# Four column groups at once in the conditioning beside the single tiles, and short vector steps of the attentions a quarter later in the order

## The chip, the cores and the metric

The kernel runs on one core of a Trainium2 chip. A core has a matrix engine (TensorE, PE in the profile, its weight loads as PEld), a vector engine (VectorE, DVE), an engine for activation functions (ScalarE, ACT), a general engine (GpSimd, POOL) and an engine that here only issues transfers (SyncE, SP). Each works through its own list of instructions in order and waits, where it must, on semaphores that the others raise. The metric is the device time of one execution in microseconds; the time before is the median of three.

## The reference

One inference step of a hybrid trunk with two layers and a model width of 2048, for 128 context tokens (`x_prompt`) and 512 latent tokens (`x_sample`) that share all weights. Cut to what matters here:

```python
def modulation(cond, w, b):                       # "conditioning": shift, scale, gate
    m = jax.nn.silu(cond) @ w + b                 # (2048) @ (2048, 6144), once for c and once for c_ctx
    return jnp.split(m, 3, axis=-1)

def rms_norm(x, g):
    return x * lax.rsqrt(jnp.mean(x * x, axis=-1, keepdims=True) + EPS) * g

for layer in range(2):
    sh, sc, gt = modulation(cond, ada_w[layer], ada_b[layer])
    h = rms_norm(x, norm_g[layer]) * (1.0 + sc) + sh
    x = x + gt * mixer(h)                         # even_mixer or odd_mixer

def even_mixer(h, ...):                           # one input projection, columns split in eight
    qa, ka, va, ga, ub, bb, cb, gb = split_cols(h @ w_in, EVEN_SPLIT)
    q, k = rms_norm(q_heads(qa), qn), rms_norm(kv_heads(ka), kn)
    o = banded_attend(apply_rope(q), apply_rope(k), v, k_ctx, v_ctx, sink)   # softmax with a sink logit
    y_a = o * silu(ga); y_b = bb * conv3(cb * ub) * silu(gb)
    return concat(y_a, y_b) @ w_out

def odd_mixer(h, ...):
    cq, ck, cv, cg, dq, dk, dv, dg = split_cols(h @ w_in, ODD_SPLIT)         # q, k: rms_norm, then rope
    o_c = rms_norm(attend(cq0, ck0, cv) - lam * attend(cq1, ck1, cv), c_on) * (1.0 - lam_init)
    y_c = o_c * silu(cg); y_d = attend(q_d, dk_all, dv_all) * silu(dg)
    return concat(y_c, y_d) @ w_out
```

The context tokens attend to themselves alone, the latent tokens to 256 cached keys and to the latent keys (in the even layer to a band of them). New keys and values of the context are outputs as well.

## The kernel before, in words

**Projections.** All activations lie transposed (features on partitions, 640 tokens along the row), each split in a high and a low part of a reduced type, and every product is three matmuls: high by high, low by high, high by low (lines 313 to 315, and 582 to 584 in the paired form). One "tile" is 128 columns of a weight matrix by 640 tokens, in two PSUM banks `pa` and `pb` of 320. Its 2048 contraction rows come in four "quarters"; a quarter is one 128x512 weight piece, loaded as `raw` by SP (line 291), split into `wh` by ACT and `wl` by DVE (`split`, lines 278 and 279), and used in 24 matmuls of 320 columns. Loads are issued five quarters ahead, splits three (`RAW_AHEAD`, `SPLIT_AHEAD`), in four buffers each.

**Stages.** A start (transposes of x, first conditioning, a lead of six tiles worked side by side), the even layer's single tiles, a tail of it with `ada_beside`, paired tiles (`run_pairs`), the output projection, the odd layer's front, its single tiles with the attentions of D and C, and its output projection.

**Slots.** After each quarter's matmuls `run_tiles` calls `slot`. It advances three kinds of generators, each by hand up to its next `yield`: `prep` (what follows a finished q, k or v tile: `q_gen`, `k_gen`, `v_gen`), `attn` (the attention of two heads: `pair_gen` for A and D, `diff_gen` for C), and `fill`, the conditioning of later use, at a `rate` of so many steps a slot. So a `yield` in a generator moves what follows it by one quarter, and the attention's short operations stand between the weight splits of the projection on the same engines.

**Planner.** What is written is a priority, not the final order: the framework's planner goes through the program with a cost for each instruction and gives each engine the first written instruction that it holds to be ready. An engine's list is then fixed. Two neighbours in the program can be apart on the engine, and where the planner's cost for an operation is too low, the engine stands at run time.

**What the change touches.** `ada_wide` (lines 233 to 250) computes conditioning of the even layer's time on DVE: 1024 columns by 16 row blocks, two multiply-adds (line 245) for each block of `ada_w`, which comes in by a 512 KB load (line 240), three buffers. `ada_on_dve` (lines 188 to 212) does the same in the odd layer in 256-column pieces (lines 204, 210). `ada_beside` (lines 252 to 275) does two blocks of 512 columns on PE while the last single tiles of the even layer run: the 16 row blocks are products with 32 columns of weights, and row block kt goes to column group kt % 4 of the array (`tile_position=(0, 32 * g)`), so that the four groups give four partial sums that are added after a transpose. Before the change a step loads two row blocks (512 KB, `w8`, four buffers) and issues two matmuls, groups 0 and 1 or groups 2 and 3.

`soft` (line 757) makes a softmax's numerators: maximum (L759), exponential with its sum `l` (L766), and the reciprocal `rl` of the sum (L772). `pair_gen` scales the numerators by it on ACT (L852) before the transposes `pt_group` (L780); `diff_gen` mixes two maps into one on DVE (L1508, L1509). `k_gen` norms and rotates a key tile: squares on ACT, mean on DVE (L655), power -0.5 on POOL (L656), products on DVE (L657 to L668), transposes back (L612 and, for the cached keys, L676). `q_gen` rotates a query tile (L702 to L705) and takes its sum of squares (L709 to L720), the power of which (L726) is used as the scale of the exponential. At the end of `diff_gen` stands the output norm: L1528 to L1535, then the transposes of `on` (L1541).

Of the kernel before, what the change touches and what calls it, by code (L numbers as in the profile page):

```python
# [20 lines left out]
P = 128  # L21
D = 2048
KT = D // P
# [26 lines left out]
FILL0 = 2.05  # L50
# [5 lines left out]
def trunk_kernel(ctx: ExitStack, tc: tile.TileContext, I: dict, O: dict):  # L56
# [30 lines left out]
    V.memset(half, -0.5)  # L87
# [100 lines left out]
    def ada_on_dve(blocks, tags, parts=1, tie=lambda: None):  # L188
# [4 lines left out]
        for l, cb in blocks:  # L193
# [3 lines left out]
            if mark is not None:  # L197
                for c in range(2):
                    V.tensor_copy(acc[c][:, 0:1], mark)
            for i in range(KT * parts):  # L200
                kt, h = i % KT, i // KT
                w = ap.tile([P, wd], F32, tag=wt[i % 3], name="adaw", bufs=bufs)
                c0 = cb * 512 + h * wd
                nc.sync.dma_start(w, I["ada_w"][l, kt * P:(kt + 1) * P, c0:c0 + wd])
# [28 lines left out]
    def ada_wide(twins):  # L233

        for l, cb in twins:
            ap = pools["cur"]
            acc = [ap.tile([P, 1024], F32, tag=f"acc{c}", name=f"acc{c}", bufs=1) for c in range(2)]
            for kt in range(KT):
                w = ap.tile([P, 1024], F32, tag="adaw", name="adaw", bufs=3)
                nc.sync.dma_start(w, I["ada_w"][l, kt * P:(kt + 1) * P, cb * 512:(cb + 2) * 512])  # L240
                for c in range(2):
# [10 lines left out]
    def ada_beside(blocks):  # L252

        for l, cb in blocks:
            acc = pS.tile([P, 1024], F32, tag="S", name="adaS")
            for k0 in range(0, KT, 2):
                w = big("w8", bufs=4).rearrange("p (k n) -> p k n", k=2)
                nc.sync.dma_start(w, ada_src(l, cb, k0, 2))
                yield
                for kt in (k0, k0 + 1):  # L260
                    g = kt % 4
                    PE.matmul(acc[32 * g:32 * g + 32, 0:512], sT[:, kt, :], w[:, kt % 2, :],
                              start=(kt < 4), stop=(kt >= KT - 4), tile_position=(0, 32 * g))
# [362 lines left out]
    def k_gen(ap, pp, tag, src, gain, new_out, vals=None, then=None):  # L626
# [28 lines left out]
        V.tensor_scalar(ss, ss, 1.0 / P, EPS, ALU.mult, ALU.add)  # L655
        G.tensor_tensor(r, ss, half[:, 0:5], op=ALU.pow)  # L656
        V.tensor_mul(kg, kg, r[:, :, None].to_broadcast([P, 5, P]))  # L657
# [12 lines left out]
        yield  # L670
# [22 lines left out]
    def q_gen(ap, pp, tag, gain, then=None, wait=True):  # L693
# [795 lines left out]
    def diff_gen(ap, h, v, kq):  # L1489
# [284 lines left out]
```

## Time and profile before

| | us |
|---|---|
| median of three runs | 2297.72 |
| lowest and highest | 2293.41, 2299.14 |
| the profiled execution, its time | 2295.01 |
| the profiled execution, its span | 2293.2 |
| PE busy in it | 2245.8 |
| DVE, ACT, POOL busy | 1685.5, 1109.8, 196.1 |

The span runs from the first to the last instruction that the profiler saw; 1.8 us of the execution's time lie around it. Busy time is the union of an engine's instructions. A group of instructions is named by its line in the kernel, engine, operation and tiles; "waits" give the time that one engine stood idle before an instruction, and which instruction ended that. A matmul's record is longer than the distance at which the next one starts, because they are pipelined, so what a matmul costs the engine is read from the distance of starts.

### The profile page before, as it was taken

Reading aid. Unit: us, or ns where it says so; the run is one execution under the profiler, and the core shown is the slowest. Engines: PE = TensorE matmul, PEld = TensorE weight load, DVE = VectorE, ACT = ScalarE, POOL = GpSimd, SP = SyncE. Lnnn points to the kernel's source line nnn. Section 1 sums busy time; section 2 is a strip of 40 time slices with the busy share of each in tenths; the row PEclk is TensorE's granted clock in tenths of the full one; section 3 lists DMA queues with packets and bytes.
Section 4 is the critical chain, followed back from the end, with each engine's and each line's share of the span. In section 5 each row is a group of like instructions: output and inputs, shape, how many; then the busy total and the mean of one; then the engine's idle time right before and its main releaser. Section 6 shows DMA issues by size and latency. Waiting matters only on the chain.

```text
span 2293.2 us, 41410 instructions
## 1 busy us (share of the span) xinstructions
PE 2245.8 (98%) x15760; PEld 2156.4 (94%) x15760; DVE 1685.5 (73%) x3188; ACT 1109.8 (48%) x2269; POOL 196.1 (9%) x273
## 2 busy tenths in 40 slices
PE   7999999999999999999999999999999999999999
PEld 5888999999889999999999999999998998999999
DVE  4659999986747778878786664857758777677665
ACT  4335553545334445444644445566665554544343
POOL 2220000000000000000100000000000101111001
PEclk9999999999999999999999999999999999999999
DMA  9985656653642325744673334422324234237541
GB/s 358 339 285 157 187 154 210 181 173 120 208 150 89 98 87 192 238 138 125 227 225 112 106 118 136 136 65 86 108 74 148 78 114 125 78 106 252 159 138 49
DMA packets 387400, 351.45 MB, mean 153 GB/s; under 512 B 17906, under 2 KB 341968, under 8 KB 386688
## 3 DMA queue, kind: packets, MB, share of 16 engines
q1 hardware_dynamic: 373360, 298.15, 42.6%
q0 software_dynamic: 12976, 48.41, 5.9%
q8 instruction: 124, 2.03, 0.3%
q10 hardware_dynamic: 864, 2.23, 0.3%
q14 instruction: 76, 0.62, 0.1%
HBM read 305.86 MB, written 42.86 MB: 152 GB/s over the span
## 4 chain that ended last, share of the span: by engine, by line
PE 84%; DVE 7%; DMA 4%; ACT 2%; issue 2%; POOL 1%; SPq 0%; ACTq 0%; POOLq 0%; DVEq 0%
PE pq L583 10%; PE pq L584 10%; PE pq L582 10%; PE pa L313 6%; PE pa L314 6%; PE pb L314 6%; PE pb L313 6%; PE pa L315 6%; PE pb L315 6%; PE T L780 2%; DMA adaw<-in_ada_w 2%; PE S L792 1%; DVE acc L210 1%; PE S L794 1%; PE S L793 1%
## 5 line engine op out<-in xcount | busy, mean ns | idle before, releaser
L278 ACT ACTIVATE wh<-raw 128x512 fp32r<-128x512 f32 (+1 forms) x400 | 240.9, 603 | 415.7 <-PE pb L314 295.7
L313 PE MATMUL pa<-h,wh 128*128 128x320 f32 x1216 | 389.4, 320 | 0.6 <-DVE z L1064 0.4
L314 PE MATMUL pa<-h,wh 128*128 128x320 f32 x1216 | 380.1, 313 | 1.4 <-DVE h L279 1.4
L315 PE MATMUL pa<-h,wl 128*128 128x320 f32 x1216 | 377.8, 311 | 2.3 <-DVE wl L279 2.3
L313 PE MATMUL pb<-h,wh 128*128 128x320 f32 x1216 | 378.2, 311 | 0.9 <-ACT h L278 0.9
L315 PE MATMUL pb<-h,wl 128*128 128x320 f32 x1216 | 377.8, 311 | 0.0
L314 PE MATMUL pb<-h,wh 128*128 128x320 f32 x1216 | 377.7, 311 | 0.0
L279 DVE TENSOR_TENSOR wl<-raw,wh 128x512 fp32r<-128x512 f32 (+1 forms) x400 | 261.7, 655 | 149.7 <-ACT wh L278 142.1
L582 PE MATMUL pq<-h,wh 128*128 128x320 f32 x896 | 277.2, 309 | 0.0
L584 PE MATMUL pq<-h,wl 128*128 128x320 f32 x896 | 276.9, 309 | 0.0
L583 PE MATMUL pq<-h,wh 128*128 128x320 f32 x896 | 276.8, 309 | 0.0
L313 PEld LDWEIGHTS pa<-h,wh 128*128 128x128 f32 x1216 | 229.3, 189 | 22.6 <-ACT wh L278 9.2
L314 PEld LDWEIGHTS pa<-h,wh 128*128 128x128 f32 x1216 | 229.7, 189 | 6.5 <-issue 4.5
L315 PEld LDWEIGHTS pa<-h,wl 128*128 128x128 f32 x1216 | 229.1, 188 | 3.9 <-DVE wl L279 2.7
L313 PEld LDWEIGHTS pb<-h,wh 128*128 128x128 f32 x1216 | 229.0, 188 | 3.3 <-issue 1.2
L314 PEld LDWEIGHTS pb<-h,wh 128*128 128x128 f32 x1216 | 229.1, 188 | 1.7 <-issue 1.7
L315 PEld LDWEIGHTS pb<-h,wl 128*128 128x128 f32 x1216 | 228.9, 188 | 0.4 <-issue 0.4
L582 PE MATMUL pq<-T,wh 128*128 128x320 f32 x672 | 208.0, 309 | 0.0
L583 PE MATMUL pq<-T,wh 128*128 128x320 f32 x672 | 207.6, 309 | 0.0
L584 PE MATMUL pq<-T,wl 128*128 128x320 f32 x672 | 207.3, 308 | 0.0
L245 DVE SCALAR_TENSOR_TENSOR acc<-adaw,sT,acc 128x1024 f32<-128x1024 f32 x150 | 188.5, 1276 | 0.0
L278 ACT ACTIVATE wh<-sx 128x512 fp32r<-128x512 f32 x168 | 105.6, 633 | 147.8 <-PE pq L583 100.0
(378 smaller groups left out, 4629.5 us busy)
## 6 DMA issues: line engine op xcount, KB each, us to landing
adaw<-in_ada_w SPq DMA_DIRECT2D x80, 512.0 KB, 3.9
raw<-in_od_w_in SPq DMA_DIRECT2D x160, 256.0 KB, 3.0
raw<-in_ev_w_in SPq DMA_DIRECT2D x130, 256.0 KB, 3.4
ada<-in_ada_w SPq DMA_DIRECT2D x11, 2048.0 KB, 13.6
adaw<-in_ada_w SPq DMA_DIRECT2D x128, 128.0 KB, 2.2
w<-in_ev_w_in SPq DMA_DIRECT2D x27, 512.0 KB, 3.8
w<-in_od_w_in SPq DMA_DIRECT2D x24, 512.0 KB, 3.8
adah<-in_ada_w SPq DMA_DIRECT2D x20, 512.0 KB, 9.7
```

Source lines behind the costliest of these rows:

```text
L210: V.scalar_tensor_tensor(out=a, in0=w, scalar=sT[:, kt, c:c + 1], in1=a, op0=ALU.mult, op1=ALU.add)
L245: V.scalar_tensor_tensor(out=acc[c], in0=w, scalar=sT[:, kt, c:c + 1], in1=acc[c], op0=ALU.mult, op1=ALU.add)
L278: A.activation(hi, x, AF.Copy)
L279: V.tensor_sub(lo, x, hi)
L313: PE.matmul(ps, wh[:, i, :], hi[:, sl], start=(j == js[0] if alone else (pos == 0 and j == 0)), stop=False)
L314: PE.matmul(ps, wh[:, i, :], lo[:, sl], start=False, stop=False)
L315: PE.matmul(ps, wl[:, i, :], hi[:, sl], start=False, stop=(j == js[1] - 1 if alone else (pos == 3 and j == 3)))
L582: PE.matmul(ps, wh[:, j, :], hi, start=(first and h == 0 and j == 0), stop=False, skip_group_check=True)
L583: PE.matmul(ps, wh[:, j, :], lo, start=False, stop=False, skip_group_check=True)
L584: PE.matmul(ps, wl[:, j, :], hi, start=False, stop=(final and h == 1 and j == 3), skip_group_check=True)
L780: PE.transpose(t[:, i * P:(i + 1) * P], p, ident)
L792: PE.matmul(d, q[0][:, bs], k[0][:, ks], start=True, stop=False)
```

## The change

- `ada_beside`: a step covers four row blocks. It needs two loads of 512 KB, the loads of the next step are issued ahead of the present step's matmuls, and its four matmuls go to column groups 0, 1, 2, 3 directly after one another. A block of 512 columns takes 6 steps of the fill in place of 10.
- `ada_wide` and `ada_on_dve`: the load of the next piece is written ahead of the multiply-adds of the present one. The fill of the even layer begins after six quarters of the single tiles and then goes at 2.1 steps a slot instead of 2.05.
- `soft` gives back numerators and sum; the reciprocal (`inverse`), the scaling in `pair_gen` and the mix in `diff_gen` are kept in a list (`later_on`) and written at the beginning of the next slot (`settle_late`), or ahead of their transposes.
- `k_gen`: the mean is taken on POOL instead of DVE, a `yield` stands between the power and the products (one of the two later ones goes), and the context's keys are transposed ahead of the latent ones. `q_gen`: the products with the tables are written after the `yield`, and the small sum `u` is read from PSUM by ACT instead of DVE, with a constant as its bias.
- `diff_gen`: the mean of the output norm is taken on POOL; the norm's product is written at the beginning of the next round (`norm`), and a `yield` follows in the last round too.

```diff
-FILL0 = 2.05
+FILL0 = 2.1
+FILL0_FROM = 6
...
-    V.memset(half, -0.5)
+    V.memset(half[:, 0:7], -0.5)
+    peps = half[:, 7:8]
+    V.memset(peps, P * EPS)
...
         for l, cb in blocks:
             acc = pS.tile([P, 1024], F32, tag="S", name="adaS")
-            for k0 in range(0, KT, 2):
-                w = big("w8", bufs=4).rearrange("p (k n) -> p k n", k=2)
-                nc.sync.dma_start(w, ada_src(l, cb, k0, 2))
+            def fetch(k0):
+                ws = [big("w8", bufs=4).rearrange("p (k n) -> p k n", k=2) for _ in range(2)]
+                for i in range(2):
+                    nc.sync.dma_start(ws[i], ada_src(l, cb, k0 + 2 * i, 2))
+                return ws
+
+            nxt = fetch(0)
+            for k0 in range(0, KT, 4):
+                ws, nxt = nxt, (fetch(k0 + 4) if k0 + 4 < KT else None)
                 yield
-                for kt in (k0, k0 + 1):
-                    g = kt % 4
-                    PE.matmul(acc[32 * g:32 * g + 32, 0:512], sT[:, kt, :], w[:, kt % 2, :],
-                              start=(kt < 4), stop=(kt >= KT - 4), tile_position=(0, 32 * g))
+                for g in range(4):
+                    PE.matmul(acc[32 * g:32 * g + 32, 0:512], sT[:, k0 + g, :], ws[g // 2][:, g % 2, :],
+                              start=(k0 == 0), stop=(k0 == KT - 4), tile_position=(0, 32 * g))
...
+    late = []
+
+    def later_on(fn):
+        f = []
+
+        def once():
+            while f:
+                f.pop()()
+        f.append(fn)
+        late.append(once)
+        return once
+
+    def settle_late():
+        while late:
+            late.pop(0)()
 
     def slot(fill=None, rate=0.0, steps=1.0):
+        settle_late()
         advance(prep, len(prep))
...
-        V.tensor_scalar(ss, ss, 1.0 / P, EPS, ALU.mult, ALU.add)
+        G.tensor_scalar(ss, ss, 1.0 / P, EPS, ALU.mult, ALU.add)
         G.tensor_tensor(r, ss, half[:, 0:5], op=ALU.pow)
+        yield
         V.tensor_mul(kg, kg, r[:, :, None].to_broadcast([P, 5, P]))
...
         V.tensor_add(m1, m1, m2)
         yield
-        yield
         drain(attn)
...
+        t = to_rows(lambda b: kg[:, b, :], False)
+        split(hi[:, CTX + NS:CTX + NT], lo[:, CTX + NS:CTX + NT], t)
         t = to_rows(lambda b: m1[:, b, :], True)
         split(hi[:, CTX:CTX + NS], lo[:, CTX:CTX + NS], t)
-        t = to_rows(lambda b: kg[:, b, :], False)
-        split(hi[:, CTX + NS:CTX + NT], lo[:, CTX + NS:CTX + NT], t)
...
-        V.tensor_mul(sw, sw, sinT)
+        yield
         m = ap.tile([P, NS], F32, tag="rp", name="qm", bufs=3)
         V.tensor_mul(m, x[:, 0:NS], cosT)
+        V.tensor_mul(sw, sw, sinT)
         V.tensor_add(m, m, sw)
-        yield
...
-        V.tensor_scalar(u.rearrange("p (j g) -> p j g", j=2),
-                        t[:, 0:192].rearrange("p (j g x) -> p j g x", j=2, g=3)[:, :, :, 0], P * EPS, None, ALU.add)
+        A.activation(u.rearrange("p (j g) -> p j g", j=2),
+                     t[:, 0:192].rearrange("p (j g x) -> p j g x", j=2, g=3)[:, :, :, 0], AF.Identity, bias=peps)
...
+        return p, l, es
+
+    def inverse(l, es=None):
+        if es is not None:
             V.tensor_add(l, l, es)
         rl = small.tile([P, 1], F32, tag="rl", name="rl")
         V.reciprocal(rl, l)
-        return p, rl, l
+        return rl
...
-            p, rl, _ = soft(ap, width, s[:, lo:hi], hi - lo, q[2][u], *sinks[j])
-            A.activation(p[:, 0:hi - lo], p[:, 0:hi - lo], AF.Copy, scale=rl)
+            p, l, es = soft(ap, width, s[:, lo:hi], hi - lo, q[2][u], *sinks[j])
+            fins.setdefault(u, []).append(later_on(
+                lambda: A.activation(p[:, 0:hi - lo], p[:, 0:hi - lo], AF.Copy, scale=inverse(l, es))))
...
+            def mix():
+                rr = [inverse(l) for l in ll]
+                w = small.tile([P, 1], F32, tag="w", name="w")
+                V.scalar_tensor_tensor(out=w, in0=ll[0], scalar=nlam, in1=rr[1], op0=ALU.mult, op1=ALU.mult)
+                V.scalar_tensor_tensor(out=pp[0][:, 0:n], in0=pp[1][:, 0:n], scalar=w, in1=pp[0][:, 0:n],
+                                       op0=ALU.mult, op1=ALU.add)
+                rls[u] = rr[0]
+            fins[u] = later_on(mix)
...
-            V.tensor_scalar(ssq, ssq, 1.0 / 256, EPS, ALU.mult, ALU.add)
+            G.tensor_scalar(ssq, ssq, 1.0 / 256, EPS, ALU.mult, ALU.add)
...
+        def norm(u):
+            V.scalar_tensor_tensor(out=ons[u], in0=ons[u], scalar=rns[u], in1=st["con"], op0=ALU.mult, op1=ALU.mult)
...
         for u in range(7):
+            if u >= 2:
+                norm(u - 2)
             if u < 5:
                 score(u, 0)
             if 1 <= u < 6:
                 groups(u - 1)
-            if u < 6:
-                yield
+            yield
             if u >= 2:
                 out(u - 2)
```

In `ada_wide` and `ada_on_dve` the line that loads becomes a function `fetch`, called once ahead of the loop and then with the next index at the head of each round.

More of the change, by code (lines that the diff above doesn't have):

```diff
@@ L237, in ada_wide, with fetch @@
             acc = [ap.tile([P, 1024], F32, tag=f"acc{c}", name=f"acc{c}", bufs=1) for c in range(2)]
-            for kt in range(KT):
+            def fetch(kt):
                 w = ap.tile([P, 1024], F32, tag="adaw", name="adaw", bufs=3)
                 nc.sync.dma_start(w, I["ada_w"][l, kt * P:(kt + 1) * P, cb * 512:(cb + 2) * 512])
+                return w
+            nxt = fetch(0)
+            for kt in range(KT):
+                w, nxt = nxt, (fetch(kt + 1) if kt + 1 < KT else None)
                 for c in range(2):
@@ L766, in soft @@
         A.activation(p[:, 0:n], s, AF.Exp, scale=rsc, bias=nm, accum_out=l)
+        es = None
         if sink is not None:
@@ L828, in groups @@
             last = len(plan(u)[4])
+            for f in fins.pop(u, ()):
+                f()
             for c0 in cs:
@@ L1504, in score @@
                 return
[L1505 removed]
+            pp, ll, _ = zip(*maps)
             maps.clear()
[L1507 to L1511 removed]
+            ps[u] = pp[0]
+            def mix():
[6 more added lines that the diff above has]
+            fins[u] = later_on(mix)
         def groups(u):
             n = len(blk_plan(u, False)[4])
+            fins.pop(u)()
             pts[u] = [pt_group(ap, [ps[u][:, i * P:(i + 1) * P] for i in range(c0, min(c0 + 4, n))])
@@ L1531, in weigh @@
             A.activation(junk, on, AF.Square, accum_out=ssq)
-            V.tensor_scalar(ssq, ssq, 1.0 / 256, EPS, ALU.mult, ALU.add)
-            rn = small.tile([P, 1], F32, tag="rn", name="rn")
+            G.tensor_scalar(ssq, ssq, 1.0 / 256, EPS, ALU.mult, ALU.add)
+            rn = rns[u] = small.tile([P, 1], F32, tag="rn", name="rn")
             G.tensor_tensor(rn, ssq, half[:, 0:1], op=ALU.pow)
-            V.scalar_tensor_tensor(out=on, in0=on, scalar=rn, in1=st["con"], op0=ALU.mult, op1=ALU.mult)
             ons[u] = on
+        def norm(u):
+            V.scalar_tensor_tensor(out=ons[u], in0=ons[u], scalar=rns[u], in1=st["con"], op0=ALU.mult, op1=ALU.mult)
         def out(u):
```

22 lines of the change are left out of this document (10 added, 12 removed).

## The prediction, made before the changed kernel was run

> **What bounds the kernel now.** I read the page's busy times and its chain first, then the table of stretches, then what PE waited for.
>
> ```profile
> PE 2245.8 (98%) x15760; PEld 2156.4 (94%) x15760; DVE 1685.5 (73%) x3188; ACT 1109.8 (48%) x2269; POOL 196.1 (9%) x273
> PE 84%; DVE 7%; DMA 4%; ACT 2%; issue 2%; POOL 1%; SPq 0%; ACTq 0%; POOLq 0%; DVEq 0%
> 146.00:587.00 441.00, 432.79 (x3085) 411.92 (x3083) 377.06 (x648) 214.37 (x474) 26.65 (x29) 1.00 0.58 177
> 587.00:664.00 77.00, 76.97 (x464) 60.66 (x464) 48.19 (x81) 21.78 (x34) 2.16 (x4) 1.00 0.63 200
> 1420.00:1760.00 340.00, 336.24 (x2381) 325.19 (x2380) 235.73 (x534) 202.48 (x416) 26.88 (x28) 1.00 0.34 102
> 1760.00:2060.00 300.00, 288.66 (x2009) 277.26 (x2009) 225.11 (x526) 154.91 (x375) 37.40 (x43) 0.99 0.33 101
> ```
>
> PE is the bound: busy 98% and 84% of the chain. (The last four lines give, for a stretch, its length and the busy time of PE, PEld, DVE, ACT and POOL, then the granted clock, DMA share and GB/s.) So a shorter time comes from two places only: less PE work, or less PE idling. 587 to 664 us is `ada_beside` among the last single tiles, and there PE never stands: whatever PE work goes there goes from the time. PE stands for 8.2 us of the even layer's single tiles (441.00 less 432.79) and, in the odd layer's, for 3.8 and 11.3 us. What it stood for, us in total, times, longest:
>
> ```profile
> PE T L612 <- DVE m L668: 7.1, 7, 1.9
> PE T L1541 <- DVE on L1535: 4.0, 3, 1.5
> PE pa L315 <- DVE wl L279: 2.3, 2, 2.0
> PE T L676 <- DVE kg L648: 2.1, 1, 2.1
> PE T L1541 <- DVE kg L648: 1.9, 2, 1.7
> PE adaS L262 <- DMA w<-in_ada_w: 0.6, 1, 0.6
> ```
>
> Rotated keys (`m`), the products before them (`kg`) and the normed output of C (`on`): 7.1 + 4.0 + 2.1 + 1.9 = 15.1 us of PE idling stand at exactly the steps that the change moves. The other 32 of PE's 47 idle us (2293.2 less 2245.8) are not at these steps.
>
> **Four column groups.** The matmuls of one step now, and the conditioning at the start, where four groups already go together (start, us, engine, line, count):
>
> ```profile
> 589.58 0.31 PE L315 MATMUL pb<-h,wl 128*128 128x320 f32 x1
> 589.82 1.05 PE L262 MATMUL adaS<-w,sT 128*32 128x512 f32 x4
> 590.80 0.41 PE L313 MATMUL pa<-h,wh 128*128 128x320 f32 x1
> 591.05 0.31 PE L314 MATMUL pa<-h,wh 128*128 128x320 f32 x1
> 591.20 0.31 PE L315 MATMUL pa<-h,wl 128*128 128x320 f32 x1
> ...
> 53.87 1.93 PE L175 MATMUL T<-ada,sT 128*32 128x256 f32 x32
> 55.73 0.42 PE L313 MATMUL pa<-h,wh 128*128 128x320 f32 x1
> L262 PE MATMUL adaS<-w,sT x64: 592/605/617, 587.0 to 663.5; 128*32 128x512 f32 x64
> ```
>
> Projection matmuls start 0.15 us apart (591.05 to 591.20). With a step between them, the second matmul after it starts 1.47 us later (589.58 to 591.05) and not 0.30: a step costs PE 1.17 us. Each written matmul is two in the trace, so the 64 are 32, 16 steps of two: 16 x 1.17 = 18.8 us.
>
> What does a step of four cost? At the start, 32 matmuls of 256 columns, eight sets of four, hold PE for 1.86 us (53.87 to 55.73): 0.23 us a set, so 0.46 us if it were 512 columns. A step of two is two sets of 512 columns in 0.98 us (589.82 to 590.80), 0.49 us a set. A set of four therefore costs no more than a set of two; the other groups ride along. Eight steps at 1.17, rounded up to 1.20 for the extra issue, are 9.6 us. **Term: 9.6 - 18.8 = -9.2 us.** The copy, transposes and reduction of a block stay.
>
> It needs its data. Two loads are now wanted for a step's matmuls, and at the first call four go out at once:
>
> ```profile
> 582.66 4.32 DMA w<-in_ada_w
> 586.50:592.00 5.50, 2.10 (x8) 0.29 (x8) 1.00 1.04 381
> w<-in_ada_w SPq DMA_DIRECT2D x12, 512.0 KB, 4.4
> ```
>
> The first 512 KB now take 4.32 us, and PE waits 0.6 us for them (above). With 381 GB/s to be had there, a second 512 KB takes 1.4 us more; were it to share with the third and fourth, 4.1 us. Could it be less than nothing? Only by the 0.6, if the planner puts the step later. **Term: +1.4 us, between -0.6 and +4.1**; I take the lower because the first two loads are first in the queue. After that a step's load is issued two steps before its use, some 9 us (a slot is about 4.7 us here: 589.82 to the next step at 594.51) against 4.4 us to land. The stage moved 200 GB/s with two loads in two slots; 1 MB a slot is 223 GB/s and the weights 56 more, under the 381 seen. So I cost the steady loads at nothing; with that cover gone, each step waits for its second load, 8 x 1.4 = 11 us. Behind these loads on SP are weight quarters, written five ahead (23 us): hidden.
>
> ```profile
> 594.51 1.05 PE L262 MATMUL adaS<-w,sT 128*32 128x512 f32 x4
> ```
>
> **Rotated keys.** `k_gen`, 12 times. The chain is: square on ACT, mean, power, product, rotation, transposes.
>
> ```profile
> L656 POOL TENSOR_TENSOR r<-ss,half x12: 1175/1280/2087, 170.3 to 2022.1; 128x5 f32<-128x5 f32 x12
> L655 DVE TENSOR_SCALAR ss<-ss x12: 158/161/165, 170.0 to 2021.8; 128x5 f32<-128x5 f32 x12
> DVE kg L657 <- POOL r L656: 13.4, 12, 1.4
> DVE acc L210 <- DMA adaw<-in_ada_w: 10.3, 15, 1.8
> 1755.73 0.49 DVE L210 SCALAR_TENSOR_TENSOR acc<-adaw,sT,acc 128x256 f32<-128x256 f32 x1 [1.79 <-DMA adaw<-in_ada_w]
> 1762.32 0.66 PE L612 MATMUL T<-ident,m 128*128 128x128 f32 x4 [1.82 <-DVE m L668]
> ```
>
> The last two rows are one case: DVE loses 1.79 us on a late piece of conditioning, then a microsecond for the power (13.4 over 12), and PE pays 1.82 us at the transposes. The change works on both: the load is written one step ahead, the product a quarter behind the power (that quarter covers the new POOL mean; I bound it by the power, 0.55 to 1.28 us as rows here show, and place it by the larger, since it has the same five columns), and the context's keys, ready first, are transposed first. Against it: the products now rank behind a weight split, and only one quarter lies between them and PE's transposes where two lay before. The rotation behind the power needs five DVE operations, some 3 us, so that quarter is just enough. I take half of what stands there: 7.1 + 2.1 = 9.2, **term -4.6 us, between -9 and +5** (as many again late, if the order is no better). The new-key transfer on POOL waits a quarter longer for `kg`; behind it are powers, on an engine busy 9%: nothing, and at most one wait of the size of the power.
>
> **Normed output of C.** 4.0 + 1.9 us of PE waits at L1541. The product comes a slot later but the transposes do too in the last round. The mean goes to POOL (20 times):
>
> ```profile
> L1534 POOL TENSOR_TENSOR rn<-ssq,half x20: 545/646/1472, 1785.4 to 2081.2; 128x1 f32<-128x1 f32 x20
> DVE on L1535 <- POOL rn L1534: 8.3, 15, 0.7
> ```
>
> DVE's 8.3 us behind the power go; the waits of PE are at the end of a head's blocks, where a yield is added. **Term: half of 5.9, -3.0 us, between -6 and +4.** That yield makes each head's generator a slot longer, and the generator is emptied by the next key tile at the latest: no cost.
>
> **Softmax tails.** 120 reciprocals, 80 scalings on ACT and 20 mixes on DVE come a quarter later:
>
> ```profile
> DVE rl L772 <- ACT p L766: 23.0, 29, 1.4
> ACT p L852 <- DVE rl L772: 34.1, 44, 2.0
> 1774.72 1.01 DVE L1509 SCALAR_TENSOR_TENSOR p<-p,w 128x768 f32<-128x768 f32 x1
> 1775.79 0.87 PE L780 MATMUL T<-ident,p 128*128 128x128 f32 x6
> ```
>
> 57 us of waits go, but on DVE and ACT; PE gains nothing of its own. What is late next is the transposes: here the mix ends at 1775.73 and they begin at 1775.79, in the middle of a quarter. There is no slack to give away, unless the planner moves the transposes too, for which it has projection matmuls to put in between. Bounds: nothing, and 20 x 1.01 = 20 us if every mix came late by itself. **Term +2 us**: nearer to nothing, because the same planner now leaves PE almost no wait there.
>
> **The rest.** `u` on ACT: 24 small reads of PSUM, and the wait for the transposes (row below) goes from DVE to ACT. Behind it on ACT stand weight splits, whose own wait for PE to free a buffer is 295.7 us; that covers it. Without it, 15 us. `q_gen`'s products have the same distance to the splits less one quarter: same cover. The fill: load ahead means that SP stands for a DVE step one piece sooner, with weight loads behind it (77.7 us of such standing before); covered by the five quarters, 4.7 us for one that isn't. The start after six quarters takes DVE work from where `kg` and `wl` cost PE 2.1 and 2.3 us (before 220 us) and puts it into a stretch in which DVE is busy 86%. **Term -0.5 us, between -3 and +3.**
>
> ```profile
> DVE u L720 <- PE T L717: 15.1, 12, 2.1
> ACT wh L278 <- PE pb L314: 295.7, 183, 4.1
> SPq L240 <- DVE acc L245: 77.7, 42, 4.7
> ```
>
> **Sum:** -9.2 + 1.4 - 4.6 - 3.0 + 2 - 0.5 = -13.9 us on the profiled execution's 2295.0, so 2281.1. That execution is 2.7 us under the median of the runs shown (2297.72); against the median, **2283.8 us**.
>
> **The rivals.**
>
> (a) *Only the column groups pay.* The order on every engine is drawn anew, and new waits take the place of the 15.1 us: 2297.7 - 9.2 + 1.4 = 2289.9 us. For it: each of those waits is a difference of a microsecond between plan and chip, and any order has some. Against it: the waits sit at few places, and all of these get more room. Chance 0.20.
>
> (b) *The tails come too late: slower.* Place: PE's transposes of `p` (L780). 100 operations (80 scalings, 20 mixes) rank behind a weight split now, and the rows at 1775 us show a slack of 0.06 us. At 0.3 us of PE wait for each, 30 us come to the sum without its +2: 2297.7 - 15.9 + 30 = 2311.8. It decides from 0.16 us each, where the 15.9 us are used up. Against it: before the change PE waits for `p` at these transposes in no row of its list. Chance 0.10.
>
> (c) *The four don't stay together.* If the planner holds the second load to be later, it puts projection matmuls between two and two; half the steps split leave 4.6 us of the 9.2: with (a), 2294.5. For it: two loads instead of one. Against: a whole slot of lead. Chance 0.06.
>
> (d) *POOL holds up DVE.* 32 small POOL operations are new. If each held DVE for its own 0.65 to 1.28 us, 12 x 1.28 + 20 x 0.65 = 28 us would come to DVE, and since they stand in the chains for which PE waited, up to as much to PE: 2297.7 - 7.8 + 28 = 2318 at most, some 2304 at half. Against it, L655 takes 158 to 165 ns in all its 12 cases, so that DVE instruction doesn't stretch; POOL's do (1175 to 2087 ns for one shape). Chance 0.04.
>
> The Trainium skill, "SBUF — State Buffer", section "Summary: rules for kernel authors", speaks for (d): with two SBUF inputs on VectorE and GpSimd reading SBUF, the second to issue is held until the first finishes. By that rule either engine can be the one held, and the sum would go up by what DVE is held; the trace agrees for POOL's spread and shows no held DVE instruction, so the rule has the chance of (d) and no term.
>
> **How the numbers follow.** My forecast has 0.60, with its own range of 2274 to 2290: up to (a), and down to where two thirds of the terms' lower spread (27.8 less 13.9 us) are had. 0.3% is about what a measurement of this kernel can tell from no change: below 2290.8 is faster, above 2304.6 slower. Forecast: faster, 0.60 of it. (a) straddles the bound by 1 us: 0.12 faster, 0.08 same. (c) same, 0.06. (b) slower, 0.10. (d) 0.02 same, 0.02 slower. Faster 0.72, same 0.16, slower 0.12. The range reaches down to 2273 and up to 2302, over (a) and (c), and leaves out (b) and most of (d).
>
> **What would show it.** PE's busy time in `ada_beside` falls by half, 16.8 us for its matmuls becoming some 8.4, eight matmuls in a row in the timeline. The waits of DVE for `l` and of ACT for `rl` nearly vanish. PE's waits at L612, L676 and L1541 (their lines will be shifted) fall from 15 to about 8 us. The prediction is wrong if PE waits for `p` at the transposes, if PE's wait for the first conditioning load grows past 4 us, if the four matmuls of a step stand apart, or if the idling of the even layer's single tiles grows beyond its 8.2 us.

## The result, and the profile after

The changed kernel takes 2276.66 us (median of four, 2276.21 to 2279.54), the kernel before on the same chip 2298.43 us. The ratio is 0.9911, with a 95% interval from 0.9893 to 0.9929: 0.9% faster, 20 us. The prediction said 2283.8, in 2273 to 2302. Its direction held and its sum came out two thirds of what was measured. The way there was partly another: the largest single gain came from a term that the prediction put at -0.5 us.

In the page of the changed kernel, first the busy times of the engines, then the chain that ended last:

```profile
PE 2237.6 (98%) x15760; PEld 2155.6 (95%) x15760; DVE 1680.4 (74%) x3133; ACT 1113.0 (49%) x2293; POOL 207.9 (9%) x305
...
PE 84%; DVE 5%; DMA 4%; ACT 3%; issue 2%; POOL 1%; SPq 0%; DVEq 0%; ACTq 0%; POOLq 0%
```

PE is busy 8.2 us less (2245.8 before) and idle 36.7 us (2274.3 less 2237.6) where it was idle 47.4. The 18.9 us by which the span shrank are these two, 8.2 and 10.7. Of the 8.2, 5.2 are at the column groups (below); PE's busy time also varies from one execution to the next, by 2.4 us between e8 and e12, which are the same kernel. The stretches that answer to those shown of before (columns as there; the even layer's single tiles, the conditioning beside them, and the odd layer's in two parts):

```profile
146.00:577.00 431.00, 428.72 (x3078) 410.54 (x3076) 374.07 (x635) 215.19 (x481) 28.59 (x31) 1.00 0.58 181
577.00:655.00 78.00, 77.54 (x507) 66.42 (x508) 52.41 (x90) 25.38 (x42) 2.16 (x4) 1.00 0.69 220
...
1405.00:1745.00 340.00, 336.12 (x2381) 325.16 (x2380) 235.34 (x524) 203.73 (x426) 30.18 (x32) 1.00 0.33 101
1745.00:2041.00 296.00, 290.27 (x2027) 278.23 (x2027) 223.04 (x498) 156.43 (x384) 44.05 (x65) 1.00 0.34 103
```

PE's idling in the even layer's single tiles went from 8.2 us to 2.3 (431.00 less 428.72), in the second part of the odd layer's from 11.3 to 5.7; in its first part nothing moved (3.8 and 3.9). What PE waited for (us in total, times, longest):

```profile
PE T L646 <- issue: 3.1, 1, 3.1
...
PE T L646 <- DVE kg L692: 1.5, 1, 1.5
PE S L831 <- ACT p L800: 1.4, 3, 0.8
PE T L646 <- DVE k1l L297: 1.3, 1, 1.3
PE T L1591 <- DVE on L1586: 1.2, 1, 1.2
...
PE T L1591 <- DVE kg L682: 1.2, 2, 1.0
PE T L819 <- DVE p L1555: 1.2, 3, 0.6
...
PE T L646 <- DVE k0l L297: 0.9, 1, 0.9
...
PE adaS L280 <- DMA w<-in_ada_w: 0.7, 1, 0.7
```

The name `m` is gone from the list, but not all of the idling at its transposes: PE still stands there for 1.3 and 0.9 us, and what ends it is now the split of the context's keys (`k1l`, `k0l`), which come first. So 7.1 us in seven waits became 2.2 us in two. The 2.1 us at the cached keys' transposes and the 2.3 us for `wl` are gone too; in the first of these two places stand 1.5 us for the normed keys (`kg` of L692), because the context's keys are transposed first. New are 1.2 us for the mixed `p` (L819, the old L780), the place where the prediction feared more. The 3.1 us near the end of the kernel, for which the profile shows no releaser, are 0.7 us before the change and 2.0 to 2.8 us in e3, e5, e6 and e7, so no one part makes them.

A better account of where time went than idle sums is the order of PE's own work. All kernels here run the same 12384 projection matmuls of 320 columns. The table gives when the n-th of them starts, less the same in the kernel before, in us; a step from one line to the next is gained or lost between these two places. (The profiled execution of the kernel before, at 2295.0, is 3.4 us under the median of its runs, so the last lines understate each kernel's gain.)

```
n       before   changed   e1     e3     e5     e4     e7     e10    e12     e9
500      144.8     -1.0    0.1    0.5    1.8    0.5    0.0    0.0    -0.3    1.1
1500     350.1     -9.0   -0.6   -7.3    1.3    1.6    1.6    1.1    -8.4   -7.8
2500     542.9     -9.5   -0.6   -6.7    0.0    1.3    1.6    1.1    -8.9   -8.4
3500     716.7    -15.4   -6.2   -6.8    0.0    1.2    1.9    1.1   -19.0  -18.6
8500    1472.9    -16.7   -3.6   -7.4   -0.8    3.3    2.8    2.5   -19.8  -20.0
10500   1947.9    -22.4   -0.8   -8.5   -4.8    2.0    3.5    2.4   -24.8  -22.1
12383   2287.9    -18.9   -1.2   -7.0   -3.3    4.7    7.3    2.8   -22.6  -22.6
```

The changed kernel gains in three places: 8.0 us between 145 and 350 us, 5.9 us at the conditioning beside the single tiles (n 2500 to 3500), and 5.7 us in the odd layer with C's heads (n 8500 to 10500).

### The profile page after: what moved, and what is told of

It is laid out like the page before. It is cut to its first block, busy times and chain, and to the rows that moved or that the text cites. A ratio compares the mean times of both kernels' runs of the same rounds, so it can differ in the third digit from the quotient of the medians.

```text
span 2274.3 us, 41403 instructions
## 1 busy us (share of the span) xinstructions
PE 2237.6 (98%) x15760; PEld 2155.6 (95%) x15760; DVE 1680.4 (74%) x3133; ACT 1113.0 (49%) x2293; POOL 207.9 (9%) x305
## 4 chain that ended last, share of the span: by engine, by line
PE 84%; DVE 5%; DMA 4%; ACT 3%; issue 2%; POOL 1%; SPq 0%; DVEq 0%; ACTq 0%; POOLq 0%
PE pq L617 10%; PE pq L618 10%; PE pq L616 10%; PE pa L331 7%; PE pb L331 6%; PE pb L332 6%; PE pa L332 6%; PE pb L333 6%; PE pa L333 6%; PE T L819 2%; PE S L831 1%; DMA adaw<-in_ada_w 1%; PE S L833 1%; PE S L832 1%; PE T L646 1%
```

## The experiments

The first four runs separate the groups from the rest, the next four do the other parts one at a time, and the last four follow up. e1 and e3 to e7 are the kernel before with one part alone, e2 is the changed kernel without one.

**e1: the four column groups alone.** Its edit is the `ada_beside` part of the diff; the loop that matters:

```diff
-            for k0 in range(0, KT, 2):
+            for k0 in range(0, KT, 4):
...
-                for kt in (k0, k0 + 1):
+                for g in range(4):
```

> The kernel before with the four column groups alone. If a set of four costs what a set of two does and the first block's steps stand apart in PE's list as in the changed kernel (11 sets instead of 16), 5 x 1.17 = 5.9 us go, all of it at the conditioning beside the single tiles, and PE's start of the later projection matmuls is early by that much: 0.26% faster. If all eight steps paid as the prediction has it, 7.8 us (0.34%). If the gain is only a redrawn order, under 2 us.

Measured: 2292.84 us against 2298.45, ratio 0.9974 (0.9964 to 0.9985), 6.0 us faster, with 5.6 us of it in the conditioning stage by the table (-0.6 to -6.2). So it is the smaller of the two forecasts. The timeline of PE in the changed kernel shows why (start, us, engine, line, count), first in the first block, then in a later step:

```profile
577.46 1.05 PE L280 MATMUL adaS<-w,sT 128*32 128x512 f32 x4 [0.66 <-DMA w<-in_ada_w]
578.44 0.41 PE L332 MATMUL pb<-h,wh 128*128 128x320 f32 x1
578.69 0.31 PE L333 MATMUL pb<-h,wl 128*128 128x320 f32 x1
578.84 0.31 PE L331 MATMUL pb<-h,wh 128*128 128x320 f32 x1
578.98 0.30 PE L332 MATMUL pb<-h,wh 128*128 128x320 f32 x1
579.12 0.31 PE L333 MATMUL pb<-h,wl 128*128 128x320 f32 x1
579.36 1.05 PE L280 MATMUL adaS<-w,sT 128*32 128x512 f32 x4
...
592.92 0.31 PE L333 MATMUL pb<-h,wl 128*128 128x320 f32 x1
593.16 1.06 PE L280 MATMUL adaS<-w,sT 128*32 128x512 f32 x8
594.15 0.41 PE L331 MATMUL pa<-h,wh 128*128 128x320 f32 x1
```

A step whose eight matmuls stand together takes 1.06 us, one of four takes 1.05: the prediction's reading of the start was right. From the start of the last projection matmul ahead of a step to the start of the second one behind it, it is 1.485 us for a step of eight and 1.472 for one of four: two more groups cost 14 ns. But in the first three of the eight steps projection matmuls stand between the two halves: the planner, it seems, held the second load to be later than the first (e8 and e12 bear this out). Eleven sets instead of sixteen are 5 x 1.17 = 5.9 us. PE's busy time at these matmuls fell from 16.8 us to 11.6 and not to 8.4 (the group's row in the changed kernel: count, busy us, mean ns, idle before):

```profile
L280 PE MATMUL adaS<-w,sT 128*32 128x512 f32 x64 | 11.6, 605 | 0.7 <-DMA w<-in_ada_w 0.7
```

**e2: everything but the groups.** The changed kernel with `ada_beside` as before the change (the same lines the other way).

> The changed kernel with the two-group conditioning of before. If the parts add up, it keeps 18.9 - 5.9 = 13 us of the gain (0.57% faster than before), and PE idles some 37 us as in the changed kernel. If the other parts need the shorter conditioning stage, or the groups bring 9 us, less: 10 us or under (0.4%).

Measured: 2284.75 us, ratio 0.9942 (0.9925 to 0.9958), 13.3 us faster. With e1's 6.0 that makes 19.3 of the 20: within the noise the groups and the rest add up, and most of the gain is not in the groups.

**e3: the vector engine's fill alone.**

```diff
-FILL0 = 2.05
+FILL0 = 2.1
+FILL0_FROM = 6
...
-                     turn=(n_turn, tail_turn, 1.0), twist=twist)
+                     turn=(n_turn, tail_turn, 1.0), twist=twist, fill_from=FILL0_FROM)
```

and `fetch` one piece ahead in `ada_wide` and `ada_on_dve`.

> The kernel before with the loads of the vector engine's conditioning one piece ahead, and its start after six quarters at 2.1 steps a slot. First theory: the 8 us that the changed kernel gains between 145 and 350 us come from here, since DVE there waited for a piece of conditioning ahead of the first key tile: 6 to 8 us faster (0.3%), with PE's wait at the transposes of the cached keys near 170 us gone. Rival: they come from the later rotation and the softmax tails, and this alone brings 0 to 2 us.

Measured: 2288.01 us, ratio 0.9955 (0.9938 to 0.9972), 10.4 us faster by the medians, the largest single part. The table has 7.8 us of it between n 500 and 1500, as much as in the changed kernel. Of PE's waits in the even layer's single tiles, this is all that is left in e3 (before the change there were also 2.1 us for `kg` and 2.3 us for `wl`):

```profile
PE T L623 <- DVE m L679: 2.0, 2, 1.1
PE pa L324 <- DVE sum L397: 0.8, 1, 0.8
```

**e10: of that part, only the loads one piece ahead.** Start and rate are as before the change.

> Of the fill's part only the loads one piece ahead; start and rate as before (first quarter, 2.05 steps). The whole part took 10.4 us off. If a late load at the head of DVE's list is what held up the first key tile and the odd layer's chains, this alone takes 6 to 10 us off. Rival: the freed first six quarters do it, and this alone takes 0 to 3 us off, all of it in the odd layer.

Measured: 2298.48 us against 2299.92, ratio 0.9996 (0.9987 to 1.0005): no change that can be told. So the gain of e3 comes with the later start and the rate. These two were not parted from each other, nor was the start run without the loads one piece ahead. DVE's list around the first key tile, before, in e10, and in e3, one fence each (start, us, engine, line; in brackets the idle time before and what ended it):

```profile
165.40 0.69 DVE L279 TENSOR_TENSOR wl<-raw,wh 128x512 fp32r<-128x512 f32 x1 [0.68 <-ACT wh L278]
168.52 0.75 DVE L243 TENSOR_SCALAR acc<-adaw,sT 128x1024 f32<-128x1024 f32 x1 [2.42 <-DMA adaw<-in_ada_w]
169.19 0.68 DVE L648 TENSOR_TENSOR kg<-T,gain_rows 128x512 f32<-128x512 f32 x1
```

```profile
165.41 0.69 DVE L289 TENSOR_TENSOR wl<-raw,wh 128x512 fp32r<-128x512 f32 x1 [0.88 <-ACT wh L288]
168.23 0.75 DVE L253 TENSOR_SCALAR acc<-adaw,sT 128x1024 f32<-128x1024 f32 x1 [2.13 <-DMA adaw<-in_ada_w]
168.90 0.68 DVE L658 TENSOR_TENSOR kg<-T,gain_rows 128x512 f32<-128x512 f32 x1
```

```profile
166.41 0.69 DVE L290 TENSOR_TENSOR wl<-raw,wh 128x512 fp32r<-128x512 f32 x1 [1.08 <-ACT wh L289]
167.25 0.69 DVE L659 TENSOR_TENSOR kg<-T,gain_rows 128x512 f32<-128x512 f32 x1 [0.15 <-ACT junk L657]
```

The very first piece of conditioning stands ahead of the first key tile on DVE, and DVE stands for its transfer while the key tile is ready. A load one piece ahead does nothing for the first piece. Starting the fill later takes it out of the place where DVE has a backlog to catch up with: DVE is busy 180.2 us between 146 and 350 us before, and 173.2 in e3. Not all of the gain is explained by this. PE's idling between 146 and 350 us fell from 6.5 us to 2.0, which is 4.5 us of the 7.8; what made the projection matmuls there come earlier by the rest was not found.

**e4: the softmax tails alone.**

```diff
-        return p, rl, l
+        return p, l, es
...
-            A.activation(p[:, 0:hi - lo], p[:, 0:hi - lo], AF.Copy, scale=rl)
+            fins.setdefault(u, []).append(later_on(
+                lambda: A.activation(p[:, 0:hi - lo], p[:, 0:hi - lo], AF.Copy, scale=inverse(l, es))))
```

and `later_on`, `settle_late`, and `mix` in `diff_gen`.

> The kernel before with the reciprocals, scalings and mixes of the softmax a quarter later, nothing else. First theory (the prediction's term): DVE's and ACT's waits for each other, 57 us, fall under 15, PE's time changes by -2 to +2 us. Rival (late tails): PE waits for p at the transposes, 100 operations at 0.16 us or more, 16 us slower. Second rival: the tails take DVE standing away from where the first key tiles and scores run, and 3 to 6 us go before 350 us.

Measured: 2299.09 us against 2298.64, ratio 1.0006 (0.9997 to 1.0015): no change that can be told, and the rival that is 16 us slower is out. But the waits that were to go did not go. In e4, DVE for ACT and ACT for DVE:

```profile
DVE rl L793 <- ACT p L782: 25.4, 31, 1.4
```

```profile
ACT p L876 <- DVE rl L793: 31.4, 40, 3.0
```

56.8 us where 57.1 were. Written a quarter later, the reciprocal stands in DVE's list mostly where it stood: of the 120, 78 start before the change with no other DVE instruction since the end of their exponential, and 73 in e4; the median distance is 0.26 us in both (the mean 0.58 and 0.78). This is what a list looks like in which the planner places the reciprocal as soon as it holds its input to be ready.

**e5: the key tiles alone.**

```diff
-        V.tensor_scalar(ss, ss, 1.0 / P, EPS, ALU.mult, ALU.add)
+        G.tensor_scalar(ss, ss, 1.0 / P, EPS, ALU.mult, ALU.add)
         G.tensor_tensor(r, ss, half[:, 0:5], op=ALU.pow)
+        yield
```

and the context's keys transposed ahead of the latent ones.

> The kernel before with the key tiles' part alone: mean on POOL, products a quarter later, the context's keys transposed first. First theory: half or more of PE's 9.2 us at these transposes goes, 4 to 7 us faster (0.2 to 0.3%). Rival: what stood there came from late conditioning and from DVE's other work, and this alone brings under 2 us.

Measured: 2291.38 us against 2298.64, ratio 0.9971 (0.9962 to 0.9980), 6.7 us faster. PE's waits at the transposes of `m`, 7.1 us in seven before, are 2.4 us in two, both now ended by the split of the context's keys (`k1l`, `k0l`). The lines at the key tiles in its list:

```profile
PE T L612 <- DVE k1l L279: 1.7, 1, 1.7
...
PE T L676 <- DVE kg L648: 1.5, 1, 1.5
...
PE T L612 <- DVE k0l L279: 0.7, 1, 0.7
```

By the table it gains in the odd layer with C's heads (n 8500 to 10500: -0.8 to -4.8) and nothing between n 500 and 1500, where e3 gains. The two are different places. What each of the three pieces (mean on POOL, later products, context's keys first) does was not parted.

**e6: the query tiles alone.**

```diff
-        V.tensor_scalar(u.rearrange("p (j g) -> p j g", j=2),
-                        t[:, 0:192].rearrange("p (j g x) -> p j g x", j=2, g=3)[:, :, :, 0], P * EPS, None, ALU.add)
+        A.activation(u.rearrange("p (j g) -> p j g", j=2),
+                     t[:, 0:192].rearrange("p (j g x) -> p j g x", j=2, g=3)[:, :, :, 0], AF.Identity, bias=peps)
```

and the products behind the `yield`.

> The kernel before with the query tiles' part alone: products behind the yield, the small sum read by ACT. First theory: no waits of PE are at these steps, so the time is within 2 us of before. Rival: the order of all engines is redrawn and new waits come or old ones go, 3 us or more either way.

Measured: 2296.49 us against 2298.64, ratio 0.9997 (0.9986 to 1.0009): no change that can be told.

**e7: the output norm alone.**

```diff
-            V.scalar_tensor_tensor(out=on, in0=on, scalar=rn, in1=st["con"], op0=ALU.mult, op1=ALU.mult)
...
         for u in range(7):
+            if u >= 2:
+                norm(u - 2)
...
-            if u < 6:
-                yield
+            yield
```

and its mean on POOL.

> The kernel before with the output norm's part alone: mean on POOL, product in the next round, one yield more. First theory: half of PE's 5.9 us at the transposes of the normed output goes, 3 us faster (0.13%), nothing before the odd layer's C heads. Rival: the last rounds come later and the wait moves to the next reader, 0.

Measured: 2297.70 us against 2298.64, ratio 0.9995 (0.9984 to 1.0005): no change that can be told. Of the waits it was to shorten, PE's at the transposes of `on` are 4.1 us where 5.9 were, but e5, which leaves the norm as it was, has 3.9 there, so the part can't be credited with it. DVE's for the power are longer:

```profile
PE T L1543 <- DVE on L1538: 3.3, 3, 1.7
...
PE T L1543 <- DVE kg L648: 0.8, 2, 0.6
```

```profile
DVE on L1538 <- POOL rn L1534: 12.6, 18, 1.6
```

DVE's were 8.3 us before. Likely the mean on POOL lengthens the chain by more than the later place of the product lets DVE do meanwhile; the two were not run apart.

**e8 and e12: the four in a row in all eight steps.** The changed kernel, with the conditioning beside the single tiles spread over more slots, which is meant to have each step's second load there in the planner's account:

```diff
-                     turn=(n_turn, tail_turn, 1.0), twist=twist, fill_from=FILL0_FROM)
+                     turn=(n_turn, tail_turn, 0.55), twist=twist, fill_from=FILL0_FROM)
```

> The changed kernel with the conditioning beside the single tiles at 0.55 steps a slot instead of 1, so that each step's second load is there and the four matmuls stand in a row in all eight steps. First theory: three more sets go, 3 x 1.17 = 3.5 us on top of the changed kernel's gain, 2273 us. Rival: the stage's end then waits for the last block or its loads, and the time is the changed kernel's or worse (2277 to 2280).

Measured: 2277.16 us, ratio 0.9909 (0.9891 to 0.9927). Its profiled execution had the conditioning stage 10.1 us shorter than before, where the changed kernel has 5.9, but it was 4 us later than the changed kernel ahead of that stage, in stages whose lists are the same. To see whether that was chance, it ran once more as e12 beside the changed kernel (e11, below).

> The changed kernel with four in a row in all eight steps, beside the changed kernel on the same chip. In one profiled execution each, the conditioning stage was 4 us shorter than in the changed kernel and the stages ahead of it, whose lists are the same, 4 us longer. If that was chance, it is now 3 to 4 us under the changed kernel (0.15%); if not, equal.

> The changed kernel once more, beside its variant with the four in a row on the same chip: 2276 to 2280 us.

Measured: e12 2275.80 us (2272.66 to 2277.88), ratio 0.9896 (0.9883 to 0.9910); e11 2277.41 us (2276.12 to 2279.17), ratio 0.9905 (0.9891 to 0.9918). In e12 PE's timeline has eight matmuls together from the first step on:

```profile
582.43 1.06 PE L280 MATMUL adaS<-w,sT 128*32 128x512 f32 x8
...
590.66 1.06 PE L280 MATMUL adaS<-w,sT 128*32 128x512 f32 x8
...
595.37 1.07 PE L280 MATMUL adaS<-w,sT 128*32 128x512 f32 x8
```

```profile
L280 PE MATMUL adaS<-w,sT 128*32 128x512 f32 x64 | 8.5, 605 | 0.0
```

The 8.5 us busy in the group's row are the half that the prediction had. The stage is again 10.1 us shorter (n 2500 to 3500: -8.9 to -19.0), against 8 x 1.17 = 9.4 by the prediction's price and the 0.6 us of waiting for the first load, which are gone from the row. So the 4.2 us over the changed kernel's 5.9 are there in the stage, in both executions. In the whole time they are not proven: the medians differ by 1.6 us, and the two kernels' runs overlap.

**e9: only the three parts that pay.** Groups (in a row), fill and key tiles; tails, query tiles and output norm as before the change.

```diff
+FILL0_FROM = 6
...
+            for k0 in range(0, KT, 4):
...
+        G.tensor_scalar(ss, ss, 1.0 / P, EPS, ALU.mult, ALU.add)
         G.tensor_tensor(r, ss, half[:, 0:5], op=ALU.pow)
+        yield
...
+                     turn=(n_turn, tail_turn, 0.55), twist=twist, fill_from=FILL0_FROM)
```

> Only the three parts that moved the time by themselves: the four column groups (at 0.55 steps a slot, so that the four stand in a row), the fill of the vector engine, and the key tiles. The softmax tails, the query tiles and the output norm are as before the change. If those three have no effect beside the others either, the time is that of the whole change, 2276 to 2278 us. If they need the others' room to pay, 2 us or more above the whole change with four in a row; if they cost, 2 us or more below.

Measured: 2272.45 us (2271.73 to 2273.93), ratio 0.9884 (0.9869 to 0.9899), the lowest of all: 5.0 us under the changed kernel beside it (e11), whose runs all lie above its own. Its busy times:

```profile
PE 2231.6 (98%) x15760; PEld 2153.9 (95%) x15760; DVE 1684.0 (74%) x3176; ACT 1108.4 (49%) x2269; POOL 198.3 (9%) x285
```

So the three other parts are not needed for the gain. Whether they cost something is open: against e12, which has them and the four in a row, the medians are 3.4 us apart, but two of e12's four runs (2272.66 and 2274.26) lie by e9's, and the profiled executions of the two end level in the table.

The parts alone, by their ratios: groups -6.0, fill -10.4, keys -6.7, tails +1.4, queries -0.7, norm -1.1, together -23.5 us; the change measured -20 and -22 beside e11. They add up within their intervals, each some 2 us either way, the fill's 4.

A column of the table is one execution, and e8 and e12, the same kernel, stand at -4.7 and -8.4 at n 1500. So here are all 13 profiled executions other than the one before, read in the same way. From n 500 to 1500 the seven with the later fill (the changed kernel, e2, e3, e8, e9, e11, e12) gain 6.3 to 8.9 us; the six without it lie between 1.9 us gained and 1.6 lost. From n 2500 to 3500 the three with eleven sets (the changed kernel, e1, e11) gain 5.6 to 5.9 us, the three with eight (e8, e9, e12) 10.1 to 10.2, and the others are within 0.3 us of before. From n 9500 to 10500, inside the odd layer, the seven with the keys' part (the changed kernel, e2, e5, e8, e9, e11, e12) gain 3.9 to 7.1 us; the six without it lie between 1.9 us gained and 1.5 lost. Each of the three parts has its own place, where every kernel that has it gains and no other gains nearly as much.

## Why the prediction was right or wrong

**The bound** was right: PE is busy 98% in both profiles, and the gain is less PE busy time and less PE idling, 8.2 and 10.7 us of span, of which 5.2 us are work that the groups took out.

**The total** came in range in part by luck. Without the term for the rest the sum is -13.4 us, and the parts that it names measured -12.4. What the change gave beyond them comes from the fill (10.4 us alone), whose own range of -3 to +3 excludes it; the range of the whole held the result only because it left room for the other terms to come out better than they did.

**Four column groups, -9.2 and +1.4.** The price of a set was right to a hundredth, 1.06 us for eight against 1.05 for four (16 x 1.17 is 18.7, not 18.8, which changes nothing); the number of sets was wrong. Eleven remained, not eight, and the stage gave 5.9 us. That is rival (c), to which the prediction gave 0.06 and half the steps: three of eight came apart. Its words against it, "a whole slot of lead", hold for the later steps, not for the first block's start, where four loads go out at once and the first three steps came apart. The term for the first load was wrong too: PE waits 0.7 us for it as it did 0.6 us, because the first half of the step needs only the first load. Of the gain 3.3 us too much, of the cost 1.4 us too much: together the step was priced 1.9 us too high. The Trainium skill, "TensorE: Matmul & The Clock Gate", section "Measured speedup vs the span model", has the span of packed matmuls as one matmul and some 4 ns for each further tile. The trace agrees that further groups cost next to nothing, but its starts are 6 to 7 ns apart.

**Rotated keys, -4.6.** Right at the edge: alone it gave -6.7 (-8.7 to -4.6 by its interval), at the step named, the transposes of `m`, where PE's idling fell by 4.7 us in e5 and by 4.9 in the changed kernel. But the prediction counted 9.2 us of waits under it, and the 2.1 us for `kg` among them did not belong there. That `kg` (L648) is the product with the gain, ahead of the mean, which the later quarter doesn't move; its wait went in e3 with the fill, and 1.5 us of it stayed in e5. By the table what the keys gain lies in the odd layer.

**Normed output, -3.0.** Not shown: -1.1, with an interval that reaches from -3.7 to +1.1. The step that failed is "DVE's 8.3 us behind the power go". They became 11.6 us in the changed kernel, although PE's waits at these transposes fell there from 5.9 us to 2.4:

```profile
DVE rl L811 <- ACT p L800: 26.4, 31, 1.6
...
DVE on L1586 <- POOL rn L1582: 11.6, 17, 1.6
```

**Softmax tails, +2.** The time was right, 1.4 us and not to be told from nothing; the mechanism was not. "57 us of waits go, but on DVE and ACT" was wrong, as the first of these rows, and ACT's 32.3 us in the row below, show. With a planner between the program and the engine's list, "a quarter later" was a priority for the reciprocals and not a place. The prediction allowed for that at PE's transposes and not on DVE.

```profile
ACT p L894 <- DVE rl L811: 32.3, 40, 2.4
```

**The rest, -0.5.** This is the term that was mis-sized: the fill gave 10.4 us, and its range of -3 to +3 did not hold it. The prediction looked at the right waits (2.1 us for `kg`, 2.3 us for `wl`, before 220 us), then put a stretch with DVE busy 86% against them as a cost. Yet nothing in the program waits for these pieces of conditioning until much later, and the stretch has room for them once the first key and query tiles are through: between n 1500 and 2500 e3 loses only 0.6 us of what it has gained. In e10, loads ahead without the later start gave nothing that can be told, where the prediction named the late load as one of the two causes in the odd layer's chains.

**The rivals.** (a) is out, since e3, e5 and e1 each pay alone and at different places. (b) is out by e4, and PE's waits for `p` are 1.2 us. (c) came in part. (d) is out: POOL has 32 more operations, and 49 DVE instructions run beside one of them; none is more than 15 ns above the median of its own line and tiles, and the 32 take 8.5 us in all. DVE's product right behind the power was not stretched either (824 to 828 ns before):

```profile
L692 DVE TENSOR_TENSOR kg<-kg,r x12: 817/824/826, 168.2 to 2000.6; 128x640 f32<-128x640 f32 x12
```

```profile
L689 POOL TENSOR_SCALAR ss<-ss x12: 193/200/503, 166.6 to 1999.1; 128x5 f32<-128x5 f32 x12
```

The rule of the Trainium skill, "SBUF — State Buffer", section "Summary: rules for kernel authors", that with two SBUF inputs on VectorE and GpSimd reading SBUF the second to issue is held, shows at most in POOL's spread, 193 to 503 ns, and in no duration of DVE here.

**The signs of being wrong.** Two of the four that the prediction named came: PE waits for `p` at the transposes (1.2 us), and the matmuls of three steps stand apart. Two did not: the first load costs 0.7 us and not 4, and the idling of the even layer's single tiles is 2.3 us. PE's waits at the steps named fell from 15.1 us to 6.1 (2.2 at `m`, 1.5 and 1.2 for `kg`, 1.2 for `on`), where it said about 8.

**Left open:** what the start after six quarters does without the higher rate or without the loads ahead, or the rate without the start; which piece of the keys' part pays; the 3.1 us near the end for which the profile names no releaser; and whether tails, queries and norm cost anything beside the other three.

## What to carry to other kernels

Work that nobody waits for soon can still cost the bound engine time, by standing at the head of another engine's list and waiting there for its own load; try to start such work behind the stage where that engine has a backlog. One more load ahead did not cure it here, because the first piece has none. Column groups rode along almost free only while they were neighbours in PE's list, so look in the timeline for whether a set stayed together: a step that needs two loads can be torn apart by whoever orders the list. And where a planner orders the lists, moving an operation in the program by a quarter may leave it where it was, as with the reciprocals; look in the engine's list before counting a gain on it.

## What the runs showed of the hardware that was not expected

The small mean on POOL takes 0.20 us on five columns (median, in the row of L689 above), where the prediction bounded it by the power's 0.55 to 1.28 us: of POOL's two operations on these columns the power is the slow one, with a median of 1.19 us in the changed kernel. The wait that was to move from DVE to ACT with the read of `u` (15.1 us before) did not appear on ACT: its 24 reads take 0.25 us each, as this row has it, and stand idle once, for 0.7 us.

```profile
L754 ACT ACTIVATE u<-T,half x24: 244/248/267, 187.3 to 1963.2; 128x6 f32<-128x6 f32 x24
```
